# Delta-rule scan of a mixer layer: four chunks' substitution in a batch, state and operands in tile pairs, second half prepared beside the scan

## The chip, the cores and the metric

The kernel runs on one core of a Trainium2 chip, as one launch. The metric is the device time of that launch in microseconds (us). The core has five engines that take their own instruction streams and wait for each other by semaphores: TensorE (PE, matmul; PEld are its weight loads), VectorE (DVE), ScalarE (ACT), GpSimd (POOL) and SyncE (SP), which here only issues DMAs. On-chip memory is SBUF with 128 partitions, and PSUM, where matmuls write.

## What is computed

A two-layer model with 256 context tokens and 256 latent tokens of width 1024. Layer 0 starts with a mixer of two scans, a state-space scan and a delta-rule scan, both in two directions; after it come a feed-forward block, attention, a mixture of experts and a second block. The change concerns the delta-rule scan of layer 0 alone. For 8 heads of 64 and each direction d it computes

```python
def _rwkv7_scan(s0, r, w, k, v, a, b):
    def step(S, inp):
        r_t, w_t, k_t, v_t, a_t, b_t = inp
        sa = jnp.einsum('bhvk,bhk->bhv', S, a_t)
        S = S * w_t[:, :, None, :] + sa[..., None] * b_t[:, :, None, :] + v_t[..., None] * k_t[:, :, None, :]
        return S, jnp.einsum('bhvk,bhk->bhv', S, r_t)
...
        kk = kk / jnp.maximum(jnp.sqrt(jnp.sum(kk * kk, axis=-1, keepdims=True)), 1e-12)
...
        rw_args = [(rh, dh[:, :, d], k_dir[:, :, d], vh, -kk, kk * ih[:, :, d]) for d in range(2)]
```

The context's last state starts the scan of the latent tokens. Decay `dh`, learning rate `ih` and key `k_dir` come from low-rank products (rank 32 per direction) of the projected input. The sum of both directions goes through a group norm, gets a bonus (r times k times v), a gate, and then the output projection.

## The kernel before

The 512 tokens are cut into 8 chunks of 64, four of the context and four of the latent part. Direction 0 takes the chunks on, direction 1 back, so the scan has 8 steps, each with one chunk each way. Within a chunk the recurrence becomes products of matrices and the inverse of a triangular matrix. Its pieces, all in `rwkv`:

- `rwkv_prep` (L627 to L672) makes for all 512 tokens the normalised key, the running sum of log decays `cs`, `b` and `kd`. The rank-32 products (L656, L663) use weights padded with zeros to a contraction of 128. The results lie in the pool `arr`.
- `products(n)` (L702) scales the operands by the chunk's decays into `ar` and `bkp`. `bkp` holds each head's 64 features in a block of its own with zeros beside it. Matmuls L731 make `g`, masked by L732; 16 transposes L739 make `bt`, copied out by ScalarE at L684, the line of every such copy.
- `base(n)` (L743) cuts 16-wide blocks out of `g` (L749, L751, L752) and inverts them by substitution: 15 rounds of a shuffle (L758), a multiplication (L761) and an addition (L763) on VectorE.
- `inverse(n)` (L765) puts the blocks onto a diagonal (L769) and doubles them twice: transposes (L774), masks on GpSimd (L777), matmuls L781 and L785, an addition (L786).
- `values(n)` (L788) brings the values to token order (L796).
- `through(n)` (L800) is the only piece with a dependence on the step before: matmuls L810 with the state X, L813, L817 with the inverse, then L824 and the state update on VectorE (L829, L830), and the readout L835. X is one tile of 128 x 4 x 128 per direction, with two heads on the diagonal of each 128 x 128.

The main loop (L846) writes `through(n)`, then `values(n+1)`, `inverse(n+1)`, `base(n+2)` and `products(n+3)`; `bonus` and `rwkv_out` (norm, bonus and gate of finished chunks) follow in later steps. Beside them up to six chunks of layer modulation per step are drawn from `ada_rest` (L377 four column groups of matmuls, L380 copy, L383 matmul, L386 addition); each needs four loads of 256 KB, into a pool of RAWS = 4 buffers. There are 26 of these chunks.

What stands in the source is not the order on the engines. A scheduler takes the instructions with the source's order as priority and lays out one fixed sequence per engine; a tile that is written again waits for its last reader, and PSUM is shared out as two banks for each of four groups (`bank`). When the scan ends, `halve` (L928) splits the result, the state-space half first, into two exact parts, and `mix_out` starts with matmul L353.

Of the kernel before, what the change touches and what calls it, by code (L numbers as in the profile page):

```python
# [85 lines left out]
def host_arrays(inp):  # L86
# [75 lines left out]
    lo = _Pack()  # L162
    for d in range(2):
        lo.add(f"w_up{d}", _rows_to(g["rw_w_up"][0, d], at=32 * d))
        lo.add(f"a_up{d}", _rows_to(g["rw_a_up"][0, d], at=64 + 32 * d))
    lo.add("g_up", _rows_to(g["rw_g_up"][0]))
    A["lora"] = lo.array()
# [14 lines left out]
    return A, pk.at, lo.at, {name: pack.at for name, pack in cst.items()}  # L182


def _consts():
    """Masks and tables that depend on the shapes alone, by the phase that uses them."""
# [54 lines left out]
# these engines take their work in the order in which it is written, where that is asked for  # L241
# [16 lines left out]
class Net:  # L258
    def __init__(self, ctx, tc, ins, at, out):
        self.tc, self.nc, self.ins, self.out = tc, tc.nc, ins, out  # L260
        self.par_at, self.lora_at, self.cst_at = at
# [23 lines left out]
    def bank(self, k, shape, i=None):  # L285
        """The PSUM banks of group k (0..3) in turn, or its bank i."""
# [23 lines left out]
    def stream(self, ctx, bufs, size=CHUNK, pairs=2, side="left"):  # L310
        """Buffers for weights as they come, and for their exact pairs."""
# [17 lines left out]
    def split(self, w, pool=None, eng=None, parts=1):  # L329
        """Exact pair of w, in parts where something else may need the engines soon."""  # L330
# [16 lines left out]
    def mm3(self, ps, w, a, wk, ak, f0, start, stop, fn=P):  # L347
        """ps += w[k].T a[k] over the blocks, as three exact single-pass products."""
# [10 lines left out]
    # -- modulation of one layer, 256 columns at a time: the blocks of c stand in four column groups of the  # L359
# [267 lines left out]
    def rwkv_prep(self, zrw, lg, arr, pool):  # L627
# [24 lines left out]
        for j in range(4):  # L652
# [18 lines left out]
            for d in range(2):  # L671
                nc.gpsimd.tensor_mul(arr["b"][:, d, j], zrw[:, j], ic[d])  # L672
# [1347 lines left out]
```

## Time and profile before

| | |
|---|---|
| median of 3 runs | 3095.95 us (3091.81 to 3096.45) |
| profiled execution, span | 3093.3 us |
| profiled execution beside the median | 2.65 us below it |
| TensorE, VectorE, ScalarE, GpSimd busy | 96%, 66%, 50%, 27% of the span |
| delta-rule stage | 233 us to 551.55 us, 10% of the span |

The profile gives, for one execution, each instruction's start and length. A busy share is an average over the whole span; where one stage changes, the windows of that stage count, and within it the waits. The mean granted clock (PEclk) is that of TensorE, as a share of its full speed. A float32 matmul shows as two records. "By line" groups join all instructions of one source line; `<-` names what released an idle engine.

### The profile page before, as it was taken

What the parts mean: (1) busy time and instruction counts of PE and PEld (TensorE: products, weight loads), DVE (VectorE), ACT (ScalarE), POOL (GpSimd) and SP (SyncE); (2) the same over time, 40 slices, a digit from 0 to 9 for tenths busy, and PEclk for the clock granted to TensorE, in tenths of its full rate; (3) what the DMA queues carried; (4) which work ended last, traced back from release to release, by engine and by line L of the source; (5) the groups of instructions that cost most, each with busy time, mean ns of one, the idle gap of its engine ahead of it and who ended that gap; (6) DMA issues with size and microseconds to landing.
All of it is one profiled execution on the core that took longest, in us unless ns stands there. A gap on an engine that the chain in (4) does not pass through costs nothing. (4 is left out here: it accounts for less than half of the span.)

```text
span 3093.3 us, 53125 instructions
## 1 busy us (share of the span) xinstructions
PE 2981.0 (96%) x22104; PEld 2678.9 (87%) x22104; DVE 2050.7 (66%) x2745; ACT 1550.3 (50%) x1831; POOL 840.8 (27%) x719
## 2 busy tenths in 40 slices
PE   7997899999999998999999999999999999999998
PEld 5884677877889778999999999989988999998998
DVE  5667987622324554898889898865696555568654
ACT  5644223432223555777777677754444444445443
POOL 0435442221122112000000000045355535454552
PEclk9998799999999999999999999999999999999999
DMA  5212234244324234999999999854633555453443
GB/s 226 69 65 69 82 111 144 103 168 156 123 76 132 96 96 172 358 352 331 357 349 333 348 333 347 314 194 159 203 128 125 174 183 189 163 192 109 147 164 126
DMA packets 132489, 585.30 MB, mean 189 GB/s; under 512 B 11792, under 2 KB 48912, under 8 KB 79760
## 3 DMA queue, kind: packets, MB, share of 16 engines
q1 hardware_dynamic: 126592, 575.35, 52.0%
q10 hardware_dynamic: 5648, 6.47, 0.9%
q8 instruction: 176, 2.88, 0.4%
q14 instruction: 73, 0.60, 0.1%
HBM read 580.73 MB, written 1.05 MB: 188 GB/s over the span
## 5 line engine op out<-in xcount | busy, mean ns | idle before, releaser
L340 DVE TENSOR_TENSOR wlo<-raw,whi 128x2048 fp32r<-128x2048 f32 (+2 forms) x497 | 1062.5, 2142 | 217.3 <-ACT whi L339 182.5
L339 ACT ACTIVATE whi<-raw 128x2048 fp32r<-128x2048 f32 (+2 forms) x500 | 889.0, 1785 | 518.7 <-PE bank L354 370.6
L353 PE MATMUL bank<-ahi,whi 128*128 128x256 f32 (+1 forms) x1904 | 507.9, 300 | 18.2 <-DVE ghi L1815 8.3
L354 PE MATMUL bank<-alo,whi 128*128 128x256 f32 (+1 forms) x1904 | 506.4, 299 | 0.9 <-DVE alo L1124 0.9
L353 PEld LDWEIGHTS bank<-ahi,whi 128*128 128x128 f32 x1904 | 368.0, 193 | 32.6 <-issue 12.4
L354 PEld LDWEIGHTS bank<-alo,whi 128*128 128x128 f32 x1904 | 368.4, 193 | 12.4 <-DVE alo L1124 2.6
L1342 PE MATMUL bank<-whi,xghi 128*128 128x256 f32 x1408 | 349.5, 286 | 0.8 <-ACT xgf L1516 0.6
L1343 PE MATMUL bank<-whi,xglo 128*128 128x256 f32 x1408 | 344.1, 282 | 0.2
L356 PE MATMUL bank<-ahi,wlo 128*128 128x256 f32 (+1 forms) x1904 | 297.9, 297 | 0.0
L354 PE MATMUL bank<-glo,whi 128*128 128x256 f32 (+1 forms) x1052 | 278.4, 299 | 1.5 <-DVE glo L1857 1.5
L1343 PEld LDWEIGHTS bank<-whi,xglo 128*128 128x128 f32 x1408 | 267.6, 190 | 1.5 <-DVE xglo L1518 1.2
L1342 PEld LDWEIGHTS bank<-whi,xghi 128*128 128x128 f32 x1408 | 267.1, 190 | 1.9 <-ACT xgf L1516 0.8
L356 PEld LDWEIGHTS bank<-ahi,wlo 128*128 128x128 f32 x1904 | 260.3, 193 | 9.6 <-issue 1.3
L1720 POOL TENSOR_TENSOR gs<-gs,gu 128x256 f32<-128x256 f32 x88 | 208.0, 2364 | 189.3 <-ACT gs L1718 189.3
L353 PE MATMUL bank<-ghi,whi 128*128 128x256 f32 (+1 forms) x924 | 244.6, 299 | 0.0
L340 POOL TENSOR_TENSOR wlo<-raw,whi 128x2048 fp32r<-128x2048 f32 x3 | 13.9, 4648 | 805.7 <-ACT whi L339 805.7
L353 PE MATMUL bank<-cathi,whi 128*128 128x512 f32 (+1 forms) x608 | 212.9, 368 | 1.4 <-ACT x L1245 1.0
L354 PE MATMUL bank<-catlo,whi 128*128 128x512 f32 (+1 forms) x608 | 211.6, 364 | 1.4 <-DVE catlo L435 1.4
L354 PEld LDWEIGHTS bank<-glo,whi 128*128 128x128 f32 x1052 | 202.3, 193 | 7.9 <-DVE glo L1857 1.9
L1345 PE MATMUL bank<-wlo,xghi 128*128 128x256 f32 x1408 | 198.3, 282 | 0.0
L353 PEld LDWEIGHTS bank<-ghi,whi 128*128 128x128 f32 x924 | 176.7, 191 | 6.4 <-DVE x L1207 0.8
L1345 PEld LDWEIGHTS bank<-wlo,xghi 128*128 128x128 f32 x1408 | 180.5, 190 | 0.3
(510 smaller groups left out, 5302.6 us busy)
## 6 DMA issues: line engine op xcount, KB each, us to landing
raw<-in_moei_dram SPq DMA_DIRECT2D x155, 1024.0 KB, 5.1
raw<-in_sfi_dram SPq DMA_DIRECT2D x88, 1024.0 KB, 4.8
raw<-in_moeo_dram SPq DMA_DIRECT2D x77, 1024.0 KB, 5.1
raw<-in_sfo_dram SPq DMA_DIRECT2D x64, 704.0 KB, 4.1
raw<-in_ada_dram SPq DMA_DIRECT2D x104, 256.0 KB, 3.6
raw<-in_smi_dram SPq DMA_DIRECT2D x24, 1024.0 KB, 4.7
raw<-in_ffi_dram SPq DMA_DIRECT2D x22, 1024.0 KB, 4.8
x<-in_moei_dram SPq DMA_DIRECT2D x21, 1024.0 KB, 5.4
```

Source lines behind the costliest of these rows:

```text
L339: self.nc.scalar.activation(like(hi, w)[:, c], w[:, c], AF.Copy)
L340: (eng or self.nc.vector).tensor_sub(like(lo, w)[:, c], w[:, c], like(hi, w)[:, c].bitcast(F32))
L353: mm(ps, l, a[0][:, ak[j]], start=start and j == 0, stop=False, skip_group_check=True)
L354: mm(ps, l, a[1][:, ak[j]], start=False, stop=False, skip_group_check=True)
L356: mm(ps, w[1][:, wk[j], f0:f0 + fn], a[0][:, ak[j]], start=False, stop=stop and j == n - 1, skip_group_check=True)
L1342: mm(ps, a[0][:, k, rows], w[0][:, k, cols], start=n == 0, stop=False, skip_group_check=True)
L1343: mm(ps, a[1][:, k, rows], w[0][:, k, cols], start=False, stop=False, skip_group_check=True)
L1345: mm(ps, a[0][:, k, rows], w[1][:, k, cols], start=False, stop=n == len(ks) - 1, skip_group_check=True)
L1720: nc.gpsimd.tensor_mul(s, s, u)
```

## The change

Only the delta-rule stage changes; what follows it is the same text.

- **Preparation in halves of 256 tokens.** `prep(0)` stands ahead of the scan; `prep(1)` is written after `through(0)` and the pieces for step 1. The rank-32 products take four row groups of the array, one for each of w and a and each direction, with an unpadded contraction of 32.
- **Products.** `bk` holds 128 features in a compact form: the two heads of a block lie in the upper and lower 64 partitions, and their matmuls alternate between the row halves of the array and two PSUM tiles. Eight transposes of 128 x 128 take the place of sixteen. The products of chunks 0 to 3 come before the scan, products n+4 in step n.
- **Substitution in batches.** `base(range(4))` inverts four chunks in one chain of 45 operations, later `base((4,5))` and `base((6,7))` two each. The cutting is done by ScalarE with eight small copies a chunk, and one addition on GpSimd.
- **Start of the inverse** on GpSimd in place of VectorE.
- **State and values** compact: X is 128 x 2 x 4 x 64, updated by two VectorE operations of 512 columns a step in place of eight of 64 x 256. Matmuls of the state, the values and the readout alternate between halves of the array (rows or columns).
- `bonus(0)` is written before the scan, `bonus(1)` and `rwkv_out` of the first half in steps 3 and 4. The tiles are in the pool of the scan itself; RAWS goes from 4 to 3.

```diff
-RAWS = 4
+RAWS = 3
...
-            for d in range(2):
-                wp = self.bank(0, [P, T])
-                mm(wp, lora[:, o[f"w_up{d}"] + j * P:o[f"w_up{d}"] + (j + 1) * P], tl, start=True, stop=True)
+            acc = [self.bank(k, [P, S]) for k in (1, 1, 2, 2)]
+            for q in range(4):
+                r = slice(32 * q, 32 * q + 32)
+                mm(acc[q], lora[r, j * P:(j + 1) * P], tl[r, at], start=True, stop=True)
...
-                nc.vector.tensor_mul(bkp[up, d, :, 0, a0], arr["b"][up, d, :, tok[d]], ei[up, d])
-                nc.gpsimd.tensor_mul(bkp[dn, d, :, 1, a0], arr["b"][dn, d, :, tok[d]], ei[dn, d])
-                nc.gpsimd.tensor_mul(bkp[up, d, :, 0, b0], arr["kd"][up, d, :, tok[d]], ei[up, d])
-                nc.gpsimd.tensor_mul(bkp[dn, d, :, 1, b0], arr["kd"][dn, d, :, tok[d]], ei[dn, d])
+                nc.vector.tensor_mul(bk[:, d, :, a0], arr["b"][:, d, :, own[d]], ei[:, d])
+                nc.gpsimd.tensor_mul(bk[:, d, :, b0], arr["kd"][:, d, :, own[d]], ei[:, d])
...
+                for j in range(4):
+                    for odd, r in both:
+                        mm(gp[odd][:, j], bk[r, d, j], ar[r, d, j], start=True, stop=True, skip_group_check=True)
...
+            for i, n in enumerate(ns):
+                for q in range(4):
...
+                    for k in range(2):
+                        nc.scalar.activation(cut[k][rq, 8 * i:8 * i + 8], G[n][q // 2][rq, :, at + 16 * k:at + 16 * k + 16],
+                                             AF.Copy, scale=self.c("half")[rq, k:k + 1])
...
-            nc.vector.tensor_mul(st.rearrange("p h (g c) -> p h g c", g=4),
+            nc.gpsimd.tensor_mul(st.rearrange("p h (g c) -> p h g c", g=4),
...
-                for j in range(4):
-                    mm(f[:, j], AR[n][:, d, j], X[d][:, j], start=j == 0, stop=False, skip_group_check=True)
...
+                    for odd, r in both:
+                        mm(f[odd][:, d, j], AR[n][r, d, j], X[r, d, j], start=d == j == 0, stop=False,
+                           skip_group_check=True)
...
+                        for odd, r in both:
+                            mm(xp[r, d, j], BT[n][:, d, j, r], uv[:, d, 4 * odd + j], start=True, stop=True,
+                               skip_group_check=True)
+                nc.vector.tensor_add(X, X, xp)
+                nc.vector.tensor_mul(X, X, WC[n][:, :, :, None].to_broadcast([P, 2, 4, 64]))
...
-        products(0)
-        base(0)
+        for _ in prep(0):
+            pass
+        for n in range(4):
+            products(n)
+        base(range(4))
         values(0)
         inverse(0)
-        products(1)
-        base(1)
-        products(2)
+        self.bonus(0, zrw, arr)
+        then = prep(1)
         for n in range(8):
             through(n)
             if n < 7:
                 values(n + 1)
                 inverse(n + 1)
-            if n < 6:
-                base(n + 2)
-            if n < 5:
-                products(n + 3)
-            if n in (3, 5):
-                self.bonus(n // 4, zrw, arr)
+            if n == 0:
+                for _ in then:
+                    pass
+            if n < 4:
+                products(n + 4)
+            if n in (1, 3):
+                base((n + 3, n + 4))
```

Three places show how the order on the engines moves. The first is VectorE in the substitution. Before, one chunk's chain (`c16`, `s16`, 8 x 15 columns in its first round) stands mixed with masking of products, scaling and the inverse of other chunks:

```order
L749 COPY c32_3277<-g1_2910 32x256 x2
L751 TENSOR_SCALAR c16_3282<-c32_3277,cst_scan_87 128x128
L752 SCALAR_TENSOR_TENSOR c16_3282<-c32_3277,cst_scan_87,c16_3282 128x128
L786 TENSOR_TENSOR st_2717<-st_2717,bank20_2784 128x512
L758 STREAM_SHUFFLE lb_3287<-c16_3282 128x8x15
L758 STREAM_SHUFFLE lb_3292<-c16_3282 128x8x14
L758 STREAM_SHUFFLE lb_3297<-c16_3282 128x8x13
L719 TENSOR_TENSOR bkp_2141<-b_1991,ei_3364 64x4x64 x2
L761 TENSOR_TENSOR lm_3289<-lb_3287,s16_3285 128x8x15
L763 TENSOR_TENSOR s16_3285<-s16_3285,lm_3289 128x8x15
```

After, the chain of chunks 0 to 3 (32 x 15 columns in its first round, here 32 x 10 and less) stands nearly alone, with one modulation addition between every ten or so:

```order
L773 STREAM_SHUFFLE lb_2425<-c16_2363 128x32x10
L776 TENSOR_TENSOR lm_2427<-lb_2425,s16_2398 128x32x10
L778 TENSOR_TENSOR s16_2398<-s16_2398,lm_2427 128x32x10
L773 STREAM_SHUFFLE lb_2430<-c16_2363 128x32x9
L383 TENSOR_TENSOR mod0_67<-bank01_3538,par_65 128x4
L776 TENSOR_TENSOR lm_2432<-lb_2430,s16_2398 128x32x9
L778 TENSOR_TENSOR s16_2398<-s16_2398,lm_2432 128x32x9
```

The cutting operations (L749 to L752) are gone from VectorE, and each shuffle needs the one before it to be used, as `lb` has one buffer.

The second place is VectorE at the state's update of step 2 of the scan, counted from 0 (L849, L850), in the changed kernel: the chain of chunks 4 and 5 (16 columns for each place of a round) has come to its end just ahead of it, and two operations of an inverse (L803, L791) stand between its rounds.

```order
L803 TENSOR_TENSOR st<-st,bank_3743 128x512
L778 TENSOR_TENSOR s_3391<-s_3391,lm 128x16x4
L773 STREAM_SHUFFLE lb<-c_3372 128x16x3
L791 STREAM_TRANSPOSE tt<-st 128x512
L776 TENSOR_TENSOR lm<-lb,s_3391 128x16x3
...
L778 TENSOR_TENSOR s_3391<-s_3391,lm 128x16
L849 TENSOR_TENSOR X<-X,bank_3664 128x512
L850 TENSOR_TENSOR X<-X,wc 128x512
```

The whole batch stands ahead of the update; before, no more than one chunk's rounds stood between two updates.

The third place is TensorE where the state enters a step. Before, full tiles of each direction stand in blocks (L810 state, L731 products, bank numbers name the PSUM tiles):

```order
L731 MATMUL bank10_2917<-ar_2890,bkp_2141 128x128 x3
L810 MATMUL bank30_3095<-X0_2137,ar_2399 128x128 x4
L810 MATMUL bank31_3109<-X1_2138,ar_2399 128x128 x4
L781 MATMUL bank21_2766<-tt_2718,lmask_2762 64x64 x16
L731 MATMUL bank11_2923<-ar_2890,bkp_2141 128x128 x4
```

After, the same step's matmuls change bank, and with it half of the array, from one to the next:

```order
L826 MATMUL bank30_3607<-X_1990,ar_2250 128x64
L826 MATMUL bank31_3608<-X_1990,ar_2250 128x64
L832 MATMUL bank30_3607<-uv_3215,g0_2266 64x64
L832 MATMUL bank31_3608<-uv_3215,g1_2267 64x64
L753 MATMUL bank10_3366<-cst_all_64,bk_3318 128x128 x4
L832 MATMUL bank31_3608<-uv_3215,g0_2266 64x64
L832 MATMUL bank30_3607<-uv_3215,g1_2267 64x64
```

## Rows read from the trace of the kernel before

**Rows 1.** The page's first part: busy time, share of the span and instructions of each engine.
```profile
PE 2981.0 (96%) x22104; PEld 2678.9 (87%) x22104; DVE 2050.7 (66%) x2745; ACT 1550.3 (50%) x1831; POOL 840.8 (27%) x719
```

**Rows 2.** Windows of the scan stage; the first line names the columns.
```profile
core 0: us, PE busy (x) PEld busy (x) DVE busy (x) ACT busy (x) POOL busy (x), PEclk, DMA share, GB/s
233.00:270.00 37.00, 26.41 (x71) 8.55 (x69) 33.52 (x35) 20.37 (x30) 14.15 (x7) 0.89 0.09 28
270.00:356.00 86.00, 69.36 (x691) 53.00 (x691) 71.29 (x261) 19.88 (x44) 47.03 (x66) 0.73 0.38 124
356.00:441.00 85.00, 74.99 (x1038) 63.97 (x1038) 77.42 (x264) 24.22 (x49) 36.46 (x48) 0.94 0.19 64
441.00:477.00 36.00, 34.84 (x460) 27.94 (x457) 31.60 (x98) 11.65 (x21) 15.56 (x20) 1.00 0.36 119
477.00:552.00 75.00, 70.10 (x926) 55.12 (x926) 51.46 (x168) 29.48 (x57) 16.24 (x21) 1.00 0.39 134
326.00:342.00 16.00, 11.21 (x136) 8.20 (x136) 15.55 (x80) 1.88 (x4) 5.61 (x7) 0.50 0.41 133
```

**Rows 3.** Timeline (start, length in us): three state updates, and the next stage's first matmul.
```profile
354.94 0.87 DVE L830 TENSOR_TENSOR X<-X,wc 64x256 f32<-64x256 f32 x2
440.33 0.86 DVE L830 TENSOR_TENSOR X<-X,wc 64x256 f32<-64x256 f32 x2
476.36 0.86 DVE L830 TENSOR_TENSOR X<-X,wc 64x256 f32<-64x256 f32 x2
551.55 0.50 PE L353 MATMUL bank<-cathi,whi 128*128 128x512 f32 x1 [0.40 <-ACT whi L339]
```

**Rows 4.** Groups of instructions by line, VectorE, 233.8 to 551.5 us.
```profile
L763 DVE TENSOR_TENSOR s<-s,lm 128x120 f32<-128x120 f32 (+14 forms) x120 | 39.1, 326 | 3.1
L761 DVE TENSOR_TENSOR lm<-lb,s 128x120 f32<-128x120 f32 (+14 forms) x120 | 38.1, 318 | 0.5
L758 DVE STREAM_SHUFFLE lb<-c 128x120 f32<-128x120 f32 (+14 forms) x120 | 26.9, 234 | 0.0
L732 DVE TENSOR_TENSOR g<-bank,cst_scan 128x512 f32<-128x512 f32 x32 | 21.6, 682 | 7.5 <-PE bank L731 7.2
L749 DVE COPY c<-g 32x256 f32<-32x256 f32 x32 | 15.6, 486 | 0.6
L830 DVE TENSOR_TENSOR X<-X,wc 64x256 f32<-64x256 f32 x28 | 15.0, 536 | 0.6
L829 DVE TENSOR_TENSOR X<-X,bank 64x256 f32<-64x256 f32 x28 | 11.7, 417 | 3.0 <-PE bank L824 2.4
L719 DVE TENSOR_TENSOR bkp<-b,ei 64x256 f32<-64x256 f32 x16 | 10.4, 664 | 4.5 <-POOL bkp L690 3.4 <-PE bank L739 0.6 <-ACT adar L380 0.5
```

**Rows 5.** Timeline around 332 us, VectorE and GpSimd.
```profile
331.24 0.23 DVE L763 TENSOR_TENSOR s<-s,lm 128x72 f32<-128x72 f32 x1
331.74 2.60 POOL L777 TENSOR_TENSOR lmask<-g,cst_scan 64x512 f32<-64x512 f32 x2 [3.47 <-PE bank L781]
331.77 1.31 DVE L763 TENSOR_TENSOR s<-s,lm 128x64 f32<-128x64 f32 x1
```

**Rows 6.** Timeline of TensorE; each float32 matmul leaves two records.
```profile
347.19 1.25 PE L817 MATMUL bank<-z,st 64*64 64x64 f32 x32
350.47 1.15 PE L835 MATMUL bank<-uv,g 128*64 128x64 f32 x16
361.72 2.05 PE L731 MATMUL bank<-ar,bkp 128*128 128x128 f32 x16
365.18 0.71 PE L739 MATMUL bank<-cst_all,bkp 64*128 64x64 f32 x16
390.07 1.16 PE L810 MATMUL bank<-X,ar 128*128 128x128 f32 x8
416.01 1.07 PE L377 MATMUL bank<-raw,c 128*32 128x256 f32 x16
```

**Rows 7.** Modulation loads, 233 to 552 us: issues of the DMA view.
```profile
raw<-in_ada_dram SPq DMA_DIRECT2D x100, 256.0 KB, 3.6
```

More of the change, by code (lines that the diff above doesn't have):

```diff
@@ L694, in rwkv, with prep @@
         S16 = {}
+        made = self.rwkv_first(lg, pool)
+        arr = {}
+        def prep(half):
+            arr.update({k: pool.tile([P, 2, 4, S], F32, name=k, bufs=1) for k in ("cs", "b", "kd")})
+            return self.rwkv_prep(half, zrw, dict(arr), made, pool)
         def tokens(n):
@@ L703, in products @@
             ch, tok = tokens(n)
+            c0, c1 = (k % 4 for k in ch)
+            own = [slice(64 * c0, 64 * c0 + 64), slice(64 * c1 + 63, 64 * c1 - 1 if c1 else None, -1)]
             ew = pool.tile([P, 2, 4, 65], F32, name="ew", bufs=1)
@@ L831, in through @@
+                nc.vector.tensor_add(X, X, xp)
+                nc.vector.tensor_mul(X, X, WC[n][:, :, :, None].to_broadcast([P, 2, 4, 64]))
+            for j in range(4):
+                for odd, _ in both:
+                    for d in range(2):
+                        mm(f[odd][second[d], d, j], G[n][d][:, 4 * odd + j, second[d]], uv[:, d, 4 * odd + j],
+                           start=False, stop=j == 3, skip_group_check=True)
             for d in range(2):
-                r1 = second[d]
@@ L843, in through @@
-                seen.add(k)
-        products(0)
-        base(0)
+                dst = y[dn if k % 4 > 1 else up, k // 4 * 2 + (k % 4 in (0, 3))].rearrange("p (j o v) -> p o j v", j=4, o=2)
+                for odd, _ in both:
+                    src = f[odd][second[d], d]
+                    if k in seen:
+                        nc.vector.tensor_add(dst[:, odd], dst[:, odd], src)
+                    else:
+                        ev(dst[:, odd], src)
+                seen.add(k)
+        for _ in prep(0):
+            pass
@@ L856, in rwkv @@
                 inverse(n + 1)
-            if n < 6:
-                base(n + 2)
-            if n < 5:
-                products(n + 3)
-            if n in (3, 5):
-                self.bonus(n // 4, zrw, arr)
+            if n == 0:
[5 more added lines that the diff above has]
+                base((n + 3, n + 4))
+            if n == 3:
+                self.bonus(1, zrw, arr)
+                self.rwkv_out(0, 0, zrw, lg, y, pool)
             if n == 4:
-                for outer in range(2):
-                    self.rwkv_out(0, outer, zrw, lg, y, pool)
+                self.rwkv_out(0, 1, zrw, lg, y, pool)
             if n == 6:
@@ L952, in layer0 @@
                 self.stream(ph, RAWS, 512, 0, "right")
-                arrp = pool(ph, "arr", side="right")
-                arr = {k: arrp.tile([P, 2, 4, T], F32, name=k) for k in ("cs", "b", "kd")}
-                with ExitStack() as c:
-                    self.rwkv_prep(zrw, lg, arr, pool(c, "pw", 2))
                 with ExitStack() as c:
                     rw = pool(c, "rw", 2)
-                    self.rwkv(zrw, arr, lg, cat[:, 0:4], rw, self.ada_rest([(0, n) for n in range(8, 24)] + [(1, n) for n in range(EARLY)], rw, 0, 1))
+                    self.rwkv(zrw, lg, cat[:, 0:4], rw, self.ada_rest([(0, n) for n in range(8, 24)] + [(1, n) for n in range(EARLY)], rw, 0, 1))
             cp = pool(late, "cp", side="right")
```

179 lines of the change are left out of this document (82 added, 97 removed).

## Prediction

> **What bounds the kernel now.** I read the busy times first: TensorE 96%, VectorE 66% over the whole span [rows 1]. That average says nothing about the stage that changes, so next come the windows of the scan [rows 2]. From 270 to 356 us VectorE is busy 71.3 of 86 us and TensorE, at a mean granted clock of 0.73, 69.4. From 356 to 441 it is 77.4 against 75.0 of 85. So until 441 us two engines share the bound, VectorE a little ahead, at a busy share of 0.9. From 441 to 477 TensorE has 34.8 of 36, from 477 to 552 it has 70.1 of 75 and VectorE 51.5: at the end TensorE bounds. The timeline gives the milestones [rows 3]: state update 0 ends at 355.8, update 3 at 441.2, update 4 at 477.2, and the projection that follows starts at 551.55. The stage starts at 233 us; all I have to find is when that projection starts after the change. Past it the two programs issue the same work in nearly the same order.
>
> **VectorE's ledger.** An operation on up to 128 partitions costs about 0.15 us and 1.04 ns per column: 72 columns took 0.23 us [rows 5], 512 columns 0.682 [rows 4].
> - *Substitution.* 360 operations (3 lines, 120 each) took 39.1 + 38.1 + 26.9 = 104.1 us [rows 4]. Columns stay the same (3 x 7680), instructions fall to 135: 225 x 0.15 = 34 us less, undisturbed. One batch costs 18.7 us for four chunks, 12.7 for two, against 9.7 for one.
> - *Cutting out the blocks* goes to ScalarE and GpSimd: L749's 15.6 us [rows 4], and two operations of 128 columns per chunk, 16 x 0.28 = 4.5 by the price above. ScalarE has 106 us of work in the 319 of the five windows [rows 2], so 64 copies of some 0.3 us are hidden there, except right ahead of the first batch, where I charge 5 us.
> - *State update.* 56 operations, 15.0 + 11.7 = 26.7 us [rows 4], become 14 of 512 columns at 0.7: 17 us less.
> - *The masked start of the inverse* moves to GpSimd: 8 x 0.7, 6 us less. It can come back as a wait. The trace shows why: while L777 ran on GpSimd from 331.74 (two pieces, 2.60 us), a 64-column L763 took 1.31 us; just ahead, a 72-column one took 0.23 [rows 5]. If each of the eight moved operations blocked one like that, 8 x 1.1 = 9 us came back, 3 more than went; between -3 and 6 I take 3, since GpSimd is idle more than half of the time [rows 2] and the batches run largely without it. The Trainium skill, page SBUF — State Buffer, section "Who interferes with whom", says that whichever of GpSimd and a VectorE operation with two SBUF inputs issues first blocks the other; the trace agrees (1.31 us), and by that rule the sum would lie nearer to -3, some 5 us later in all.
> - *Added:* preparation in halves, 40 more small operations, 6 us; four more readout additions or copies a step, hidden on whichever engine is free.
> Together roughly 70 (34 + 20 + 17 + 3 - 6) of the 265 us that VectorE is busy here [rows 2]. Not all of it is on the path.
>
> **TensorE's ledger.** An ungrouped record of 128 columns takes 2.05/16 = 0.13 us, one of 64 columns 1.15/16 = 0.07 [rows 6]. Two things show what parts of the array side by side give: L817, whose matmuls alternate between two quadrants, needs 1.25/32 = 0.04 for 64 columns, and L377, four column groups, 1.07/16 = 0.07 for 256 columns [rows 6]. The change puts products, state, values and readout into that form: about 15 us of a step's 20 (L731 4.1, L810 2.3 and so on). If halves run beside each other, 7.6 us of a step go, if not, none. Counting the instructions of the new order by these prices, TensorE's work from update 0 to the projection is 127 us paired and 177 unpaired; before, 180 in the three windows [rows 2]. I take three quarters of the saving, since columns show it plainly (L377) and rows less so: L739 alternates rows and needs 0.71/16 = 0.04 [rows 6].
>
> **The stage, leg by leg.**
> 1. *To update 0: 345 against 355.8.* Only half of the preparation stands ahead: VectorE's 33.5 us [rows 2] become some 17, done at 254. But four chunks' products must now be ready before any substitution. They share one bk buffer and two PSUM tiles, so each waits for the transposes of the one before; I put one at 10 us, between 4.4 (its own VectorE work: two ar, two bk, four L732 of 0.68 [rows 4]) and 13 (the same chain at a granted clock of 0.50, as at 326 [rows 2]): done at 294. Cutting 5, batch 19 with 4 of other work between, 322. First inverse 15, 337, first pass through the state 8, 345. Bounds 322 to 356.
> 2. *Update 0 to 4: 111 us against 121.4.* Here the order matters: update 1 stands behind the whole second half of the preparation (16.5 us) and products of chunk 4, update 2 behind the batch of chunks 4 and 5, update 4 behind that of 6 and 7. My sums of undisturbed VectorE work are 62.7 us to update 3 and 27.9 to update 4; before, 69.7 and 29.3, which took 85.4 and 36.0. At the same ratio (1.23): 77 and 34. TensorE has 84 to 120 us of work in this leg, so it would decide only where nothing is paired.
> 3. *Update 4 to the projection: 53 us against 74.4.* VectorE has only 18 us here. TensorE makes no products and no bonus any more here: 43 us of work paired, 57 unpaired, 46 as I take it; 4 us of gaps, about what it has in the last window [rows 2]. Three more: the exact halves of the state-space result, which were made in the shadow before, now lie in room that the last readout still holds, and start after it.
>
> Sum: 345 + 111 + 53 = 509 against 551.6, **43 us less**. What is hidden: modulation loads (3.6 us each, four a chunk [rows 7]; three buffers in place of four lengthen a chunk's cycle from about 5 to 6 us, but 12 chunks have 164 us after update 0, and 14 before it over 110 us). If that cover goes, 26 x 6 = 156 us still fit the 276. The profiled span is 3093.3 us, 2.7 below the median of runs, 3095.95; 3095.95 - 43 = **3053 us**.
>
> **Rivals.**
> - *More comes off:* VectorE runs at 0.9 busy as undisturbed work instead of 0.81, TensorE fully paired, products at 6 us each. To update 0 at 329, then 100, then 48: 477, 75 us less, 3021. For it: L761 and L763 lose time to GpSimd now [rows 5], and there will be 90 of them in place of 240. Against: the inverse keeps its four mask operations on GpSimd, and gets a fifth.
> - *Halves don't run beside each other* (the change doesn't do what it says on TensorE): 177 us of work plus 16 of gaps after update 0 and 3 for the halves instead of 164, and 345 becomes 347: 543, 9 us off, 3087, between 3075 and 3102. For it: at 350.47 the K=128 readout of 64 columns has 0.07 a record [rows 6], no less than full width would need. Against it L377.
> - *Slower: TensorE's clock.* Where TensorE has gaps, the granted clock is 0.50, its lower level of 1.2 GHz: 326 to 342 us, 11.2 busy of 16 [rows 2]. From 441 on, without gaps, it is 1.00. Less work on TensorE with the same VectorE chains means more gaps. If the low level held through legs 2 and 3, 135 us of work would become 270, more than the 207 that there are (164 + 43): it decides when the mean clock of these legs falls below 135/207 = 0.65. At 0.55 they take 245: 345 + 245 = 590, 38 us slower, 3134. The Trainium skill, page TensorE: Matmul & The Clock Gate, Part 1, says that throttling is the default and activity releases it: a rule against this change; the trace agrees so far as 0.50 goes with the gaps at 326. Against: TensorE would still be busy 0.82 of legs 2 and 3, and 0.88 (75.0 of 85) held 0.94.
>
> **How the numbers follow.** Forecast (3035 to 3075) 0.55, more 0.20, halves not paired 0.15, slower 0.10. Of the third, two thirds are faster by over 0.2% (6 us, about what can be told from no change here): faster 0.85, same 0.05, slower 0.10. The range leaves out the slow case, the end of the third and little of the second: 3005 to 3090.
>
> **What would show it.** Right: update 0 at 335 to 350 us, substitution in three batches of 19, 13 and 13 us, 14 state updates, TensorE's X matmuls (L826) and readout (L854) near 0.04 us a record, granted clock above 0.9 after update 0, the projection near 509. Wrong: L826 or L854 at 0.07, a granted clock of 0.5 to 0.7 between update 0 and 4, or update 0 later than 356, because products at over 12 us each hold up the batch.

## The result, and the profile after

The changed kernel takes **3129.58 us** (median of 4 runs, 3126.69 to 3135.42) against 3094.3 of the kernel before (4 runs): ratio 1.0120, 95% interval 1.0105 to 1.0134. It is 35 us slower; 3053 was forecast, with a range that ended at 3090. In the changed file the lines up to L400 stand three higher: L374 is the L377 of before, L380 the L383, L383 the L386, L350 the L353 of the projection.

The page's first part of the changed kernel, which answers [rows 1]: VectorE has 69 us less to do, TensorE 11 us more, and the span is 3126.9 us.

```profile
PE 2992.2 (96%) x22328; PEld 2671.3 (85%) x22328; DVE 1981.7 (63%) x2385; ACT 1590.1 (51%) x1948; POOL 827.0 (26%) x699
```

The windows of the scan stage, columns as in [rows 2], with one window more since the stage now reaches 590 us:

```profile
233.00:270.00 37.00, 28.76 (x161) 14.68 (x161) 24.93 (x42) 18.78 (x38) 11.86 (x19) 0.68 0.33 108
270.00:356.00 86.00, 61.31 (x396) 39.17 (x398) 45.45 (x112) 25.36 (x66) 20.88 (x27) 0.66 0.31 104
356.00:441.00 85.00, 75.26 (x990) 52.52 (x983) 47.32 (x82) 45.73 (x94) 39.16 (x44) 0.80 0.18 61
441.00:477.00 36.00, 31.18 (x392) 26.30 (x394) 27.22 (x81) 10.80 (x26) 11.08 (x14) 0.64 0.12 38
477.00:552.00 75.00, 69.17 (x947) 51.21 (x944) 35.67 (x110) 28.72 (x62) 22.06 (x26) 0.85 0.28 95
552.00:590.00 38.00, 27.47 (x535) 23.15 (x534) 18.03 (x41) 16.67 (x34) 6.89 (x8) 0.93 0.35 128
```

From 270 to 356 us, where both engines were near their limit before, VectorE is busy 45 of 86 us and TensorE 61. Less work is done in more time, so something waits. The milestones, which answer [rows 3] (timelines of VectorE and TensorE, start and length, updates 0, 3 and 4 and the next stage's first matmul):

```profile
373.72 0.69 DVE L850 TENSOR_TENSOR X<-X,wc 128x512 f32<-128x512 f32 x1
484.27 0.69 DVE L850 TENSOR_TENSOR X<-X,wc 128x512 f32<-128x512 f32 x1
525.42 0.69 DVE L850 TENSOR_TENSOR X<-X,wc 128x512 f32<-128x512 f32 x1
589.75 0.80 PE L350 MATMUL bank<-cathi,whi 128*128 128x512 f32 x1 [5.47 <-ACT whi L336]
```

Update 0 ends at 374 (forecast 345), update 4 at 526 (456), the projection starts at 590 (509). The three legs miss by 29, 41 and 11 us: 81 in all, of which 38 are a real loss against before (551.55) and 43 the gain that never came.

**What TensorE waits for.** The waits of TensorE from 233 to 552 us (us in total, times, longest), first two rows of the changed kernel:

```profile
PE bank L374 <- DMA raw<-in_ada_dram: 22.5, 18, 2.7
PE bank L746 <- DVE g L748: 7.3, 4, 3.4
```

and the row of the same transfer in the kernel before:

```profile
PE bank L377 <- DMA raw<-in_ada_dram: 1.6, 2, 1.2
```

So the modulation loads, which the forecast had hidden, keep TensorE waiting for 22.5 us. The timeline of TensorE during the first batch of substitution shows the pattern; a chunk is four quarters of four matmuls each, one load each:

```profile
338.48 1.07 PE L374 MATMUL bank<-raw,c 128*32 128x256 f32 x4 [1.87 <-DMA raw<-in_ada_dram]
340.09 1.01 PE L380 MATMUL bank<-cst_all,adar 128*128 128x2 f32 x4 [0.54 <-ACT adar L377]
341.36 1.08 PE L374 MATMUL bank<-raw,c 128*32 128x256 f32 x8 [0.25 <-DVE mod L383]
342.62 1.07 PE L374 MATMUL bank<-raw,c 128*32 128x256 f32 x4 [0.17 <-DMA raw<-in_ada_dram]
345.60 1.07 PE L374 MATMUL bank<-raw,c 128*32 128x256 f32 x4 [1.92 <-DMA raw<-in_ada_dram]
```

Three quarters run at once, the fourth waits 1.9 us: with three buffers its load can only be issued when the first quarter has been used. The next chunk's L380 follows 7.1 us after the one shown. VectorE shows the other side, four modulation additions: three between the rounds of the same batch, the fourth just behind its last round:

```profile
334.05 0.16 DVE L383 TENSOR_TENSOR mod<-bank,par 128x4 f32<-128x4 f32 x1 [2.14 <-PE bank L380]
341.14 0.16 DVE L383 TENSOR_TENSOR mod<-bank,par 128x4 f32<-128x4 f32 x1 [2.19 <-PE bank L380]
348.26 0.16 DVE L383 TENSOR_TENSOR mod<-bank,par 128x4 f32<-128x4 f32 x1 [2.16 <-PE bank L380]
355.44 0.16 DVE L383 TENSOR_TENSOR mod<-bank,par 128x4 f32<-128x4 f32 x1 [3.31 <-PE bank L380]
```

An addition of 0.16 us, put into the fixed order of VectorE, holds up the chain behind it for over 2 us each time; the three inside the batch wait 6.5 us together. The Trainium skill, page PSUM — Partial Sum Buffer, section "Engine vs sequencer instructions", says that VectorE's queue is strictly first in, first out; the trace agrees, since rounds whose operands had long been there stood behind the first three. The batch runs from 322.86 to 352.1 us, 29 us where 23 were forecast.

### The profile page after: what moved, and what is told of

It reads as the page before. It is cut to its first block, busy times and chain, and to the rows that moved or that the text cites. A ratio compares the mean times of both kernels' runs of the same rounds, so it can differ in the third digit from the quotient of the medians.

```text
span 3126.9 us, 53310 instructions
## 1 busy us (share of the span) xinstructions
PE 2992.2 (96%) x22328; PEld 2671.3 (85%) x22328; DVE 1981.7 (63%) x2385; ACT 1590.1 (51%) x1948; POOL 827.0 (26%) x699
## 5 line engine op out<-in xcount | busy, mean ns | idle before, releaser
L350 PE MATMUL bank<-ahi,whi 128*128 128x256 f32 (+1 forms) x1904 | 508.4, 300 | 19.1 <-DVE ghi L1838 8.3
L350 PEld LDWEIGHTS bank<-ahi,whi 128*128 128x128 f32 x1904 | 367.8, 193 | 33.2 <-issue 12.2
L353 PE MATMUL bank<-ahi,wlo 128*128 128x256 f32 (+1 forms) x1904 | 297.6, 297 | 0.0
L353 PEld LDWEIGHTS bank<-ahi,wlo 128*128 128x128 f32 x1904 | 259.5, 192 | 9.8 <-issue 1.3
L350 PE MATMUL bank<-ghi,whi 128*128 128x256 f32 (+1 forms) x924 | 244.6, 299 | 0.0
L350 PE MATMUL bank<-cathi,whi 128*128 128x512 f32 (+1 forms) x608 | 212.5, 367 | 6.4 <-ACT whi L336 5.5
L350 PEld LDWEIGHTS bank<-ghi,whi 128*128 128x128 f32 x924 | 176.7, 191 | 6.4 <-DVE x L1230 0.8
```

Of the source, the lines that this page charges most:

```text
L350: mm(ps, l, a[0][:, ak[j]], start=start and j == 0, stop=False, skip_group_check=True)
L353: mm(ps, w[1][:, wk[j], f0:f0 + fn], a[0][:, ak[j]], start=False, stop=stop and j == n - 1, skip_group_check=True)
```

## The experiments

Times are medians with the ratio to runs of the kernel before on the same chip and its 95% interval; "projection" is the start of the next stage's first matmul. The first theory was that going from four buffers to three costs most; the rivals were the second half of the preparation, the batching, and TensorE's clock.

**e1: the changed kernel with four buffers.** The pool is full to the last bytes, so one small tile shares the place of another.

```diff
-RAWS = 3
+RAWS = 4
-        nrm = pool.tile([8, S], F32, name="nrm", bufs=1)
+        nrm = pool.tile([P, 32, 16], F32, name="lb", bufs=1).rearrange("p a b -> p (a b)")[0:8, :S]
```

> The changed kernel with four load buffers (RAWS 4) as before; the 1 KB tile of key norms shares another tile's place to make room. Theory 'loads' (a chunk needs four loads, with three buffers TensorE stops in its order at the fourth until it lands: 18.5 us of such waits before the first state update and 6.6 after, against 1.6 before the change): these waits fall under 5 us, the first update comes 12 us or more earlier than 374, and the whole takes 20 to 35 us less, 3095 to 3110. Rival 'clock' (TensorE's lower clock costs it whatever the loads do): waits go but the time stays within 10 us of 3130. Rival 'lead-in' (four products and a batch stand in series): first update stays at 365 or later.

Measured: 3098.92 us, ratio 1.0033 (1.0021 to 1.0045). The projection starts at 559.6 instead of 589.8. The wait of TensorE for these loads:

```profile
PE bank L374 <- DMA raw<-in_ada_dram: 3.3, 4, 1.5
```

Of the loss of 1.20%, 0.87% (27 us) go with the one buffer. Waits and time came as the theory 'loads' said; update 0 came at 364.2, 10 us sooner, just short of the 12 expected. The granted clock of the whole execution stays about what it was (0.965 after, 0.967 here). Within the stage it rose from 270 to 356 us, where the waits had been (0.66 to 0.81), but from update 0 to the projection it fell (0.81 to 0.77), and there the other 20 of the projection's 30 us went. So most of this part was not the clock.

**e2: the kernel before with three buffers.**

```diff
-RAWS = 4
+RAWS = 3
```

> The kernel before with three load buffers and nothing else. Theory 'loads': it becomes 15 to 35 us slower than before, with waits for modulation loads on TensorE of 20 us or more in the stage. Rivals 'clock', 'lead-in' and 'second half' (the second half's preparation on the path): within 8 us of before, since none of what they name is here.

Measured: 3120.02 us, ratio 1.0091 (1.0074 to 1.0108): 28 us, the same price on the other kernel. The 20 us of load waits on TensorE that were expected did not come (7.1 us from 233 to 552); here the price shows at another place. The last state update ends at 540.1, 2.5 us later than before; but the chunks are not done (timelines of VectorE and TensorE):

```profile
539.23 0.87 DVE L830 TENSOR_TENSOR X<-X,wc 64x256 f32<-64x256 f32 x2
545.97 0.16 DVE L386 TENSOR_TENSOR mod<-bank,par 128x4 f32<-128x4 f32 x1 [0.48 <-PE bank L383]
553.41 0.16 DVE L386 TENSOR_TENSOR mod<-bank,par 128x4 f32<-128x4 f32 x1 [1.83 <-PE bank L383]
560.60 0.16 DVE L386 TENSOR_TENSOR mod<-bank,par 128x4 f32<-128x4 f32 x1 [2.39 <-PE bank L383]
567.86 0.16 DVE L386 TENSOR_TENSOR mod<-bank,par 128x4 f32<-128x4 f32 x1 [7.09 <-PE bank L383]
574.86 0.15 DVE L386 TENSOR_TENSOR mod<-bank,par 128x4 f32<-128x4 f32 x1
578.86 0.79 PE L353 MATMUL bank<-cathi,whi 128*128 128x512 f32 x1 [4.08 <-ACT whi L339]
```

Five chunks at 7.2 us follow the last state update, where before the last one was done at 515. The projection comes 4 us after the last. So the cover of these loads is not the length of the stage divided by their number: they get their turn in TensorE's fixed order, and what does not fit there comes at the end.

**e3: the changed kernel with the loop of before** (three buffers; substitution one chunk at a time, products three ahead).

```diff
-        for n in range(4):
-            products(n)
-        base(range(4))
+        products(0)
+        base((0,))
...
+            if n < 6:
+                base((n + 2,))
```

> The changed kernel with the loop of before: substitution one chunk at a time, products of three chunks ahead, the second half's preparation after step 0. Theory 'lead-in': the first update comes at 335 to 350 in place of 374 and the whole takes 15 to 25 us less. Theory 'loads': the first update moves by less than 10 us, the whole by less than 10 either way, as VectorE gets 90 operations of substitution back.

Measured: 3127.16 us, 1.0124 (1.0097 to 1.015). Update 0 comes at 337, 37 us sooner than in the changed kernel, and all of it is given back: projection at 584.2, TensorE's wait for loads 15.1 us. The first update came as 'lead-in' said, the time as 'loads' said: an early start of the scan is worth nothing here.

**e4: no second half of the preparation** (left out; the later products read the first half's arrays).

```diff
-        then = prep(1)
...
-                for _ in then:
-                    pass
+                pass
```

> The changed kernel without the preparation of the second half of the tokens (left out: its norms, low-rank products, running sums; the later products read the first half's). Theory 'second half': the step from update 0 to update 1 falls from 50 us to about 29, as before the change, and the whole takes 20 us or more less. Theories 'loads' and 'clock': the work is mostly beside other work, the whole takes under 12 us less.

Measured: 3110.1 us, 1.0061 (1.0041 to 1.0081), 18 us off the changed kernel, between what the two theories said (20 or more; under 12). Update 0 to update 1 takes 18 us instead of 50. The gain is the size of prep(1)'s whole work (16.5 us in the forecast), but VectorE has idle time there (in the changed kernel it is busy 47 of 85 us from 356 to 441), which made the order of the work the next suspect.

**e5: e1, and the products of the state update in another PSUM group.** In e1 the state's values are in place (ScalarE, L694) at 389 us; yet the matmuls that need them, L847, come at 416.77. Timeline of TensorE, then of VectorE, in e1:

```profile
416.19 0.66 PE L753 MATMUL bank<-cst_all,bk 128*128 128x128 f32 x4
416.77 1.15 PE L847 MATMUL bank<-uv,bt 128*64 128x64 f32 x32
418.18 0.67 DVE L849 TENSOR_TENSOR X<-X,bank 128x512 f32<-128x512 f32 x1
```

L847 takes its tile from PSUM group 1, whose two banks go round in the order of the source. prep(1) and products(4), which the source writes ahead of `through(1)`, use the same group, so the update stands behind all of them.

```diff
-                xp = self.bank(1, [P, 2, 4, 64])
+                xp = self.bank(0, [P, 2, 4, 64], 0)
```

> The changed kernel with four load buffers, and the product for the state's update (L847) in a PSUM bank of group 0 in place of group 1. Theory 'PSUM turn' (the update's product takes its turn in group 1 behind all tiles of the second half's preparation and of chunk 4's products, as these are written ahead of it): update 1 follows update 0 by under 35 us in place of 55, and the whole takes 8 us or more less than with four buffers alone (3099). Theory 'ScalarE' (the second half's preparation is slow on its own, through table loads and waits for its sigmoids): update 1 may come earlier, but the products of chunk 4 and all that hangs on them stay where they are, and the whole moves by less than 5 us.

Measured: 3093.0 us, 1.0001 (0.9991 to 1.0011). The timeline in e5:

```profile
386.70 1.20 ACT L694 ACTIVATE uv<-bank 64x512 f32<-64x512 f32 x2
388.31 0.18 PEld L847 LDWEIGHTS bank<-uv,bt 128*64 128x64 f32 x1
395.23 0.86 DVE L850 TENSOR_TENSOR X<-X,wc 128x512 f32<-128x512 f32 x1
549.25 0.79 PE L350 MATMUL bank<-cathi,whi 128*128 128x512 f32 x1 [5.14 <-ACT whi L336]
```

L847 starts 0.4 us after its values, update 1 ends at 396.1 instead of 419.6, the projection starts at 549.3 instead of 559.6. These are the other 10 us by the ratios (1.0033 to 1.0001; the medians alone differ by 6, as the kernel before ran at 3090.38 beside e1 and at 3093.16 beside e5). In this order of the work, buffer and PSUM group together are the whole loss: 27 + 10 = 37 of 1.20% = 37 us. That brings the changed kernel level with the one before; the 43 us that were forecast are still missing.

**e6 and e7: is the batching worth something?** e6 is e3 with four buffers (the substitution's tiles are cut to one chunk's size to make room), e7 has the group of e5 as well.

```diff
-RAWS = 3
+RAWS = 4
...
-                xp = self.bank(1, [P, 2, 4, 64])
+                xp = self.bank(0, [P, 2, 4, 64], 0)
```

> The loop of before (substitution one chunk at a time, second half's preparation after step 0) with four load buffers. Theory 'lead-in', now that no load waits stand in the way: first update near 335, the whole 10 us or more below 3099. Theory 'second half': what the earlier first update gains is given back in the next two steps, the whole within 6 us of 3099.

> The same with the state's product in group 0. Theory 'PSUM turn': 10 us or more below the loop of before with four buffers. Theory 'ScalarE': within 5 us of it.

Measured: e6 3112.43 us, 1.0067 (1.0051 to 1.0084), projection 572.8; e7 3125.67, 1.0107 (1.0090 to 1.0124), projection 583.7. e1 beats e6 by 0.34%, though update 0 comes at 364 there and at 342 in e6: the loop with batches is the better one, and both theories of e6, which put it at 3105 or less, failed. e6 differs from e1 in more than the batches (products and second half stand elsewhere), so the 0.34% are the loop's. e7 is a miss: the group that gives 10 us in the order of e5 costs 12 in that of e3. The same bank of group 0 also takes the tiles of the values' transposes (L808) and of the products with the inverse (L837). In e7 the values' matmuls wait 4.6 us for the update, but in e5 they wait as long; so where the 12 us arise stays open.

**e8: does more work on TensorE bring its clock up?** Ahead of each K=32 matmul of the preparation stands one over the whole array, whose result is overwritten.

```diff
+                mm(acc[q], self.c("ident"), zrw[:, 8 + j, at], start=True, stop=True, skip_group_check=True)
                 mm(acc[q], lora[r, j * P:(j + 1) * P], tl[r, at], start=True, stop=True, skip_group_check=True)
```

> The changed kernel with four load buffers, and ahead of each low-rank matmul (contraction 32) a matmul of the same 256 columns over the full array whose result is overwritten: 32 more matmuls, 64 records, 15 us of TensorE at full clock. Theory 'clock' (TensorE loses its clock in the preparation, where matmuls use a quarter of the array's rows, and this costs the stage more than the work itself): the granted clock from 240 to 285 us and from 370 to 410 rises above 0.9, and the time stays or falls below 3099. Rival: the clock rises or not, and the time grows by 5 to 20 us, as the clock there decides little.

Measured: 3127.77 us, 1.0095 (1.0063 to 1.0127). The first window of the stage, e1 and then e8:

```profile
233.00:285.00 52.00, 38.52 (x274) 21.76 (x272) 33.16 (x56) 28.11 (x58) 19.45 (x33) 0.72 0.38 127
```
```profile
233.00:285.00 52.00, 49.45 (x218) 24.69 (x218) 23.84 (x45) 23.33 (x43) 11.46 (x19) 0.64 0.31 101
```

and two windows after it, e1 and then e8:

```profile
360.00:400.00 40.00, 38.60 (x421) 24.56 (x415) 18.96 (x35) 28.47 (x52) 14.82 (x19) 0.77 0.18 60
400.00:440.00 40.00, 32.85 (x449) 27.06 (x448) 28.09 (x66) 17.64 (x43) 18.27 (x21) 0.76 0.18 54
```
```profile
360.00:400.00 40.00, 39.10 (x529) 25.10 (x530) 15.89 (x26) 18.04 (x35) 15.85 (x14) 0.93 0.22 74
400.00:440.00 40.00, 38.24 (x250) 22.24 (x250) 16.53 (x31) 20.08 (x39) 12.98 (x17) 0.59 0.21 70
```

In the first window TensorE is busy 49 of 52 us instead of 39 and its granted clock is lower, 0.64; later it is higher once (0.93 for 0.77) and lower once (0.59 for 0.76), with the scan some 10 us further back. In neither window that the theory named did the clock rise above 0.9 (0.58 from 240 to 285, 0.80 from 370 to 410), so what the clock itself costs here remains untested. The Trainium skill, page TensorE: Matmul & The Clock Gate, Part 1, says that activity releases the throttle; by the busy times of the first window the trace disagrees, and of the two later ones one agrees and one does not.

**e9 to e12: parts of the change in the kernel before.** e9 has the compact state, values and passes through the state; e10 also the compact products (with two buffers of `bk`, where the change has one); e11 is e10 with the update in PSUM group 0; e12 is e10 with the cutting on ScalarE and GpSimd. The core of each:

```diff
-                    for r in (up, dn):
-                        nc.vector.tensor_add(xn[r, :, r], xn[r, :, r], xp[r, :, r])
-                        nc.vector.tensor_mul(xn[r, :, r], xn[r, :, r], wc[r].to_broadcast([64, 4, 64]))
+                nc.vector.tensor_add(X, X, xp)
+                nc.vector.tensor_mul(X, X, WC[n][:, :, :, None].to_broadcast([P, 2, 4, 64]))
...
-                        mm(gp[:, j], bkp[:, d, j, odd], ar[:, d, j], start=True, stop=True, skip_group_check=True)
+                        mm(gp[odd][:, j], bk[r, d, j], ar[r, d, j], start=True, stop=True, skip_group_check=True)
...
-                nc.vector.tensor_copy(c32[rq], G[n][q // 2][rq, :, at:at + 32])
+                    nc.scalar.activation(cut[k][rq], G[n][q // 2][rq, :, at + 16 * k:at + 16 * k + 16],
+                                         AF.Copy, scale=self.c("half")[rq, k:k + 1])
```

> The kernel before with one part of the change: compact state, values and passes through the state in tile pairs, and nothing else (four load buffers, whole preparation ahead, substitution chunk by chunk, products as before). By the prediction's ledgers this takes 17 us from VectorE and, for column halves alone, about 4 us a step from TensorE. Theory 'halves pair': 10 to 30 us less than before. Theory 'clock' (less work only makes TensorE's clock fall): within 6 us of before.

> The same with the compact products as well (row halves alternating, eight transposes in place of sixteen, two 128-partition operations on GpSimd in place of six of 64). Theory 'halves pair': 5 to 15 us below the state alone. Theory 'clock': no gain over the state alone, with a lower granted clock after update 0.

> As the state and products parts together, with the product for the state's update in group 0 of PSUM. Theory 'PSUM turn': 5 us or more below those two alone. Rival: group 0 holds the values and the inverse's product, so the turn only moves there, and the time stays within 4 us or grows.

> State and products parts together with the cutting of the blocks on ScalarE and GpSimd. By the ledger 20 us of VectorE work go. Theory 'VectorE bounds until update 3': 8 to 18 us below state and products alone. Rival: the copies come later than VectorE's own did (a wait for ScalarE and GpSimd ahead of each substitution) and the time stays within 5 us.

| | time | ratio, interval | update 0 | projection | granted clock, 356 to 552 |
|---|---|---|---|---|---|
| e9 | 3095.67 | 1.0005 (0.9994 to 1.0015) | 349.4 | 552.4 | 0.86 |
| e10 | 3095.1 | 1.0003 (0.9993 to 1.0013) | 344.3 | 548.5 | 0.92 |
| e11 | 3100.18 | 1.0021 (1.0012 to 1.0031) | 342.7 | 558.0 | 0.83 |
| e12 | 3090.36 | 0.9986 (0.9976 to 0.9996) | 333.8 | 547.6 | 0.83 |

Update 0 comes 6 to 22 us sooner than in the kernel before (355.8). Of e12's 22 us, 4 reach the projection (551.55), and the time is 0.14% lower. The gains that 'halves pair' and 'VectorE bounds until update 3' put on e9, e10 and e12 did not come. Theory 'clock' named the times of e9 and e10, and all four show a lower granted clock than the kernel before (0.97), though e10's is above e9's; that the clock is the cause is not shown by this. e11 is again a miss of the PSUM group: what helps in one order hurts in another.

**e13 to e15: what holds the end?** Two causes were tried for the vanishing of earlier starts: the modulation chunks, or the scan's own chain. e13 is e12 with a fifth buffer, in the room that the compact operands leave. e14 (on e12) and e15 (on e5) move six of the 26 chunks into a later stage.

```diff
-RAWS = 4
+RAWS = 5
...
-EARLY = 10
+EARLY = 4
```

> The kernel before with compact state, values and products and the cutting on ScalarE and GpSimd (as e12, 3090.36 us), RAWS 5 in place of 4. If the loads of the modulation bound the end of the scan: the chunks end earlier than 510 us, the next stage starts 5 to 15 us before 547.6 and the time falls to 3075 to 3085 us. If the scan's own chain or TensorE bounds it: the start of the next stage within 3 us of 547.6 and 3088 to 3093 us.

> As e12, with 20 modulation chunks beside the scan in place of 26 (EARLY 4 for 10); the other six come with the rest of layer 1's, in a later stage. Nothing is left out. If the chunks bound the end of the scan: six chunks of about 5 us each are gone from it, next stage at 515 to 530 us in place of 547.6; the total then shows what the six cost later. If the scan's own chain bounds it: next stage at 540 to 548 us, since only the six chunks' TensorE work (6 x some 1.5 us) goes.

> The changed kernel with RAWS 4 and the update's products in PSUM group 0 (as e5, 3093.0 us), with 20 modulation chunks beside the scan in place of 26. If the chunks bound here too: next stage at 515 to 535 us in place of 549.3 and a time below 3085 us unless the six cost as much later. If after update 0 the changed kernel is bound by its own chain (its last chunk was done 47 us before the next stage): next stage at 543 to 550 us and 3088 to 3098 us.

Measured: e13 **3084.15 us**, 0.9975 (0.9966 to 0.9985); e14 3090.71, 0.9998 (0.9989 to 1.0007); e15 3106.06, 1.0048 (1.0034 to 1.0062). The projection's first matmul in the timelines of e13, e14 and e15:

```profile
543.14 0.50 PE L353 MATMUL bank<-cathi,whi 128*128 128x512 f32 x1 [1.32 <-ACT whi L339]
```
```profile
542.63 0.50 PE L353 MATMUL bank<-cathi,whi 128*128 128x512 f32 x1 [1.58 <-ACT whi L339]
```
```profile
551.14 0.80 PE L350 MATMUL bank<-cathi,whi 128*128 128x512 f32 x1 [5.46 <-ACT whi L336]
```

Six chunks less bring 5 us at the projection in e14 (547.6 in e12) and nothing in e15 (549.3 in e5). So at four buffers the chunks do not bound the end of the scan. What is left is the scan's own chain, with TensorE on it: in e15 TensorE is busy 38.6 of the 40 us from 360 to 400 although the last chunk was done at 360. That is an exclusion and not a test, and it does not tell a long chain from a low clock: in e15 the granted clock is 0.77 from 356 to 552, in e5 0.82. What the six chunks gave, they cost in their new place, in e15 14 us more by the ratios, which neither of its theories named; where, was not followed. The fifth buffer of e13 brings 4.4 us at the projection, between what the loads' theory (5 to 15) and no effect (within 3) would have brought, and 0.11% in the ratio, within the intervals of e12 and e13. Yet e13, which is three parts of the change and one buffer more instead of one less, is the fastest of all: 0.25% under the kernel before, and 1.4% under the changed one (0.9975/1.0120 = 0.9857).

## Why the prediction was wrong, step by step

- **"What is hidden: modulation loads"** was the step that failed most, 27 us (e1), 28 on the other kernel (e2). The forecast put three buffers at 6 us a chunk and compared a sum, 26 x 6 = 156, with 276 us of room. A chunk takes 7.1, and the sum was the wrong question: the chunks stand in fixed places between the scan's instructions on TensorE and VectorE, so each late load is a wait of both engines (22.5 us on TensorE), or, as in e2, moves chunks behind the scan.
- **"Update 1 stands behind the whole second half of the preparation (16.5 us)"** was priced as VectorE's work. The price is a PSUM tile: from update 0 to update 1 e1 takes 55 us, e5 33. The forecast did not ask in which order a group's tiles come free. 10 us.
- **"Only half of the preparation … done at 254"**: VectorE's last operation of it ends at 268, 1.1 us sooner than that of the whole one before (L670, 269). Its VectorE work did shrink (24.9 us in the first window, 33.5 in [rows 2]). ScalarE loads its function tables 13 times in the stage, 5 times before, at 1.28 us each, because the pieces mix functions. In e5 the preparation also ends late, at 270, and VectorE's operations wait 12 us for ScalarE from 233 to 268 (2 us before). That the table loads alone delay the end was not tried. 14 us.
- **Products at 10 us**: 268 to 320 us makes 13 each, the upper end that the forecast named. But with four buffers they take 10.9 each in e1 (269.9 to 313.4) and 10.4 in e5 (270.2 to 311.9). So these 12 us are for the most part the price of the first step once more, and 10 was about right. What leaves e5's update 0 at 363.5, 18.5 later than forecast, is the late preparation and the batch (315.2 to 342.5: 27 us for 23).
- **Undisturbed VectorE work times 1.23** for update 0 to 4: this leg takes 131 us in e5, 111 were forecast. The VectorE work did go (56.0 busy of 85 us from 356 to 441 in e5, 77.4 before), and TensorE took the bound, at a lower clock. Windows of e5, to be held against [rows 2]:

```profile
356.00:441.00 85.00, 75.38 (x1002) 56.96 (x997) 56.03 (x125) 47.76 (x98) 35.28 (x44) 0.80 0.12 38
441.00:477.00 36.00, 30.62 (x477) 25.54 (x475) 27.22 (x64) 16.34 (x36) 18.60 (x19) 0.81 0.11 37
477.00:549.00 72.00, 63.62 (x1102) 52.21 (x1101) 39.65 (x112) 33.00 (x71) 21.38 (x26) 0.87 0.24 83
```

  TensorE is busy 170 of 193 us, VectorE 123. The forecast let TensorE decide this leg "only where nothing is paired". What the clock does to a piece of work shows in sixteen records of L374 in e5, at a granted clock of 0.50, where the same work took 1.07 us at 1.00 [rows 6]:

```profile
386.44 1.93 PE L374 MATMUL bank<-raw,c 128*32 128x256 f32 x16
```

  Busy time weighted by the granted clock is an estimate of TensorE's work: 75.38 x 0.80 + 30.62 x 0.81 + 63.62 x 0.87 = 140 us in e5, and 74.99 x 0.94 + 34.84 + 70.10 = 175 before [rows 2]. So the work shrank about as forecast (from 180 to 139.5 with three quarters of the saving), but at the lower clock it filled 170 us, 163 of them after update 0, where the forecast had 164 for these legs in all. At the 0.97 of before the 140 would be 145 us. By this estimate the lower clock is worth some 25 of the missing 43 us, if TensorE bounds these legs; no run changed the clock alone, so this cause stays open.
- **Update 4 to the projection, 53 us**: 55 in e5. Right, once buffer and PSUM group are mended.
- **Halves beside each other, three quarters of the saving**: right for the column halves, and for the row halves of the products, wrong for the row halves of the state. Timeline of TensorE in the changed kernel:

```profile
376.39 1.55 PE L826 MATMUL bank<-X,ar 64*128 64x64 f32 x22
379.91 0.88 PE L826 MATMUL bank<-X,ar 64*128 64x64 f32 x10
413.51 1.21 PE L746 MATMUL bank<-ar,bk 64*128 64x128 f32 x16
445.15 1.15 PE L847 MATMUL bank<-uv,bt 128*64 128x64 f32 x32
446.14 1.10 PE L854 MATMUL bank<-uv,g 128*64 128x64 f32 x32
```

  Column halves pair: L847 and L854 need 0.036 us a record, against 0.07 for the readout of before [rows 6]. The row halves of L746, with 128 moving columns, need 1.21 us for 16 records, against 2.05 for L731 [rows 6]. The row halves of L826, with 64, need 2.43 us for 32 records, no less than L810's 16 records at 1.16 us for eight [rows 6]. Yet L739, transposes that alternate row halves with 64 moving columns, took 0.04 a record [rows 6]; what sets L826 apart was not followed. The Trainium skill, page TensorE: Matmul & The Clock Gate, Part 3, says that loading weights overlaps running matmuls only where the row groups differ. They differ in L746 and in L826, and the trace shows a gain in the first and none in the second.
- **The slow rival** named 3134 us and 590 for the projection, and 3129.6 and 590 came. That is the right number by luck, for another reason. Its condition was a mean clock below 0.65 after update 0; the windows above give about 0.81 from 356 to 590 us ((85 x 0.80 + 36 x 0.64 + 75 x 0.85 + 38 x 0.93)/234), and e1 and e5 take the loss away with 0.77 and 0.82 from update 0 to the projection. The clock did fall (0.97 in the same legs before), and it may be why the saved work is not seen in e5; that is not shown. The bound of 0.65 was also the wrong one to ask for: 135/207 is where the whole gain is gone, but the forecast itself had only 164 us for these legs, and 135/164 = 0.82 is where TensorE begins to take from it. (With three quarters of the saving the 135 should be 139.5.)

Two of the three signs of being wrong came: L826 at 0.07, and update 0 after 356 with products at 13 us. The chances failed with the steps: 0.85 for faster rested on two savings that were real (VectorE's 69 us, update 0 early in e9 to e12) and did not lie on the path.

## What to carry to other kernels

Before a change takes a buffer from a stream, follow one turn of the stream in the trace: how many loads a piece needs, when the last of them may be issued, and which engines stand behind it in order; a sum of transfer times against the length of the stage does not answer that. When a piece of work is written ahead of a step on the critical chain, list every shared pool that both use, PSUM groups first, since the later one gets its tile last even if its engine is idle. Test the move to another group, too: it gained 10 us in one order of the work (e5) and cost 12 and 6 in two others (e7, e11). And test a saving alone in the old kernel: an earlier milestone that does not reach the end of the stage is no gain.

## What was not expected of the hardware

- More work on TensorE did not bring a higher granted clock throughout: 0.64 at 49.45 busy of 52 us (e8) against 0.72 at 38.52 (e1), and 0.59 at 38.24 of 40 against 0.76 at 32.85, but 0.93 at 39.10 against 0.77 at 38.60. In the changed kernel it stands at 0.50, its level of 1.2 GHz, through stretches in which TensorE is busy without a gap; two windows, columns as in [rows 2]:

```profile
392.00:400.00 8.00, 8.00 (x58) 4.01 (x55) 4.91 (x8) 6.81 (x11) 3.49 (x5) 0.50 0.29 99
472.00:480.00 8.00, 8.00 (x90) 6.70 (x90) 2.56 (x4) 4.02 (x9) 6.03 (x7) 0.50 0.16 55
```

  The forecast read 0.50 as the mark of gaps; a busy TensorE in the profile is no sign of the upper level.
- Column halves with 64 moving columns double the rate (0.036 us a record, L847 and L854, against 0.07). Row halves gain with 128 moving columns (L746, 0.08 against 0.13) and not in L826 with 64 (0.07).
- One late load in four reaches VectorE: where TensorE waits 1.9 us for it, the addition of 0.16 us waits 2.14 to 2.19 us inside the batch. With loads in time (e1) it waits at most 1.32 us there.
